# All 128 chunks of U computed ahead of V in the PEER layer

## The chip, the cores and the metric

The kernel runs on one core of a Trainium2 chip. Time is device microseconds; the time given for a kernel is the median over its runs. A profile is one more execution, taken with the hardware profiler. The engines are PE (TensorE, the matmuls; PEld is its weight loading), DVE (VectorE), ACT (ScalarE), POOL (GpSimd) and SP (SyncE, which here only issues DMAs).

## The reference, cut to what matters

The whole computes two blocks of a network on 512 tokens of width 1024: a mixer (neighbourhood attention and a gated linear recurrence) and a PEER layer, and then a second block of convolution, attention and two feed-forward layers. The change is in the PEER layer, with one piece in the mixer. In the PEER layer each token chooses, in each of 8 heads, 16 of 16384 experts by product keys, and sums their outputs:

```python
q = (t @ wq).reshape(PEER_BLOCK, PEER_HEADS, 2, PEER_DQ // 2)
s = jnp.einsum('tpcd,pckd->tpck', q, sub_keys).astype(jnp.float32)
s1, i1 = lax.top_k(s[:, :, 0], PEER_TOPK)
s2, i2 = lax.top_k(s[:, :, 1], PEER_TOPK)
...
top, pos = lax.top_k(cand, PEER_TOPK)
idx = jnp.take_along_axis(cidx, pos, axis=-1)
g = jax.nn.softmax(top, axis=-1)
a = jax.nn.gelu(jnp.einsum('tpkd,td->tpk', u[idx], t).astype(jnp.float32), approximate=False)
return jnp.einsum('tpk,tpkd->td', (g * a).astype(t.dtype), v[idx])
```

## The kernel before, in words

The first 128 tokens (`T0`) are done as the reference says, by gathering: for every token the rows of U, and then of V, of its 128 experts are fetched. POOL issues an indirect DMA for 128 rows of 4 KB (one expert of each token, 512 KB), and DVE multiplies it with the token's input and sums (U, line 1155), or adds it, weighted, to the output `accg` (V, line 1160). There are 256 such tiles, five buffers for them (`GBUFS`), and each is asked for three ahead of its use.

The other 384 tokens (`TD`) are done densely. The experts lie in 128 chunks of 128. For chunk e, `hidden` (line 1335) loads U's part of 512 KB on SP's queue into one of four `w` buffers, splits it into a high and a low half (ACT makes `wh`, DVE `wl`), and makes 24 matmuls of 384 columns: three products (high by high, high by low, low by high) for each of eight pieces of the contraction. ACT takes the GELU of the result, the tile `act`, 128 x 384. For the second half of the layer, `operands` (line 1360) multiplies `act` by the routing weights of the chunk (`Wr`, on DVE), splits the result (`sh`, `sl`), loads V's part of 512 KB into a `w` buffer and splits it (`vh`, `vl`). `products` then makes 18 matmuls of 512 columns into six banks of PSUM that gather the sum over all chunks.

The order is this. While the routing is computed (`route`: `topk`, mostly DVE, and `spread`, which builds for each of the 384 tokens a matrix of routing weights with small matmuls and stores them to DRAM as `Wd`), PE computes U's chunks ahead of need: `ahead` computes `AHEAD` = 116 chunks and stores each `act` to DRAM (`Ad`, line 1357, on ACT's queue). `weave` (line 64) decides the order by costs: it always takes the next step of that generator whose summed costs are smallest. A step of `ahead` costs `PACE` = 2.95, a step of `spread` 1.45, two gathered tiles `GATHER` = 11; `topk` of one block of 128 tokens comes to 47.6, `spread` of one to 46.4. `merge` joins the `topk` of block t and the `spread` of block t-1, and their costs add up. `REST` = 4 of the 116 chunks come after the weave. PE's order is the one written there; on the other engines and on SP's queue a planner orders the instructions by their place in the program and by when it expects them to be ready.

Then comes the V stage (the loop in `peer`, line 1064 on): for e from 0 to 127 the operands, a share of the gathering that is left (spread over the first 120 chunks), and the products of chunk e - `OPS_LAG` (2). For e below 116 the `act` is loaded back from `Ad` (line 1368), into one of three buffers; the last 12 chunks call `hidden` there. `Wr` holds the weights of `GROUP` = 8 chunks. It is loaded whole at the first chunk of a group, 1536 KB in pieces of 512 bytes (line 1365), into one of two buffers. The split halves have `TAIL + OPS_LAG` = 4 buffers each. The last two chunks' products are held back and made bank by bank.

Three more things are touched. `late_mods` computes the columns of four modulation vectors on DVE (`mod_chunk`, line 324, from 32 parts of `wmt` loaded on SP's queue through the `w` buffers), while the mixer's first projection runs on PE. `rows_of` (line 363) makes of such a column vector a row that lies in all 128 partitions, by multiplying the identity with it on DVE (`dg`) and with a matrix of ones on PE. And the layer's input, `h2` (32 KB of each partition), lies lowest on the right side of SBUF until the V stage is done, because `hidden` is still called there; what the gathering needs (`pg`) lies above it, and the V stage's pool `pm` above that.

## Time and profile before

| | |
|---|---|
| median of 3 runs | 3147.87 us (3142.14 to 3153.35) |
| the profiled execution | 3142.09 us, of which its span is 3140.3 us |
| mean granted clock of TensorE | 0.974 |
| PE, PEld | busy 94% and 81% of the span |
| DVE, ACT, POOL | busy 60%, 40%, 13% |
| DMA | 537.8 MB, mean 171 GB/s |

The page cuts the span into 40 equal slices, 78.5 us each. PE counts as busy also where a matmul waits in its pipeline, so the steps between the starts of matmuls say more. A DMA share of 1.00 means that the core's 16 DMA engines were busy all the time; packets that overlap can bring it above. In the view by stretches, a number in brackets is the count of instructions. A line as `1601.98 0.96 PE ... x2 [3.57 <-ACT vh L132]` means two instructions from 1601.98 us on, ahead of which the engine was idle for 3.57 us, until ACT's `vh` released it.

### The profile page before, as it was taken

The page shows a single profiled execution, that of the slowest core. Times are in us where ns is not written, and L with a number is a line of the kernel's source. Part 1 is how long each engine was busy: PE and PEld are TensorE (multiplying, and loading weights), DVE is VectorE, ACT ScalarE, POOL GpSimd, SP SyncE. Part 2 cuts the span into 40 slices and gives each one's busy share as a digit, 9 for nine tenths or more (in the row PEclk, how much of TensorE's full clock was granted, in tenths as well). Part 3 has the DMA queues.
Part 4 walks back from the last instruction along what each step waited for, and adds up shares of the span by engine and source line. Part 5 has one row for each costly group of instructions (what it writes and reads, how often), then busy time and mean ns, then how long its engine had stood idle before and what let it go on. Part 6 is the DMA issues. An engine that isn't in the chain of part 4 may idle for free.

```text
span 3140.3 us, 42392 instructions
## 1 busy us (share of the span) xinstructions
PE 2951.1 (94%) x16073; PEld 2529.5 (81%) x16073; DVE 1898.6 (60%) x3680; ACT 1268.6 (40%) x2275; POOL 401.1 (13%) x398
## 2 busy tenths in 40 slices
PE   7998999999999999898888888899999999999998
PEld 5887887799899999776676767778888887788887
DVE  5744497549999856678788875544433245543323
ACT  4233463343466778522232323432423234433222
POOL 2100000001111110133344431000000000000000
PEclk9999999999999999999999998999999999999999
DMA  6622202236676776899999995222333322123332
GB/s 250 228 64 72 62 1 81 98 126 202 204 239 218 255 248 225 286 353 358 355 363 360 361 353 201 64 72 94 100 95 94 99 86 65 54 88 94 99 103 81
DMA packets 257166, 537.79 MB, mean 171 GB/s; under 512 B 20161, under 2 KB 135105, under 8 KB 252609
## 3 DMA queue, kind: packets, MB, share of 16 engines
q1 hardware_dynamic: 196512, 345.82, 33.8%
q0 software_dynamic: 36864, 134.23, 12.0%
q10 hardware_dynamic: 23584, 55.03, 4.6%
q8 instruction: 126, 2.06, 0.3%
q14 instruction: 80, 0.65, 0.1%
HBM read 484.93 MB, written 50.08 MB: 170 GB/s over the span
## 4 chain that ended last, share of the span: by engine, by line
PE 56%; DVE 19%; DMA 9%; issue 4%; ACT 1%; POOL 1%; SPq 0%; DVEq 0%; ACTq 0%; POOLq 0%
PE bank L121 54%; DMA act<-Ad 7%; DVE wl L1343 2%; DVE gr L1155 2%; DVE accg L1160 2%; DVE vl L134 2%; DVE sl L134 1%; PE bank L608 1%; DVE act L1372 1%; PE bank L1471 1%; DVE idx L1275 1%; DVE tmp L1233 1%; DVE eq L1272 1%; DVE eq L1274 1%; DVE KX L802 1%
## 5 line engine op out<-in xcount | busy, mean ns | idle before, releaser
L121 PE MATMUL bank<-hh,wl 128*128 128x512 f32 (+2 forms) x2304 | 837.0, 364 | 41.8 <-DVE wl L1343 32.3
L121 PE MATMUL bank<-hh,wh 128*128 128x512 f32 (+2 forms) x2304 | 843.0, 367 | 16.2 <-ACT wh L1342 6.8
L121 PE MATMUL bank<-hl,wh 128*128 128x512 f32 (+2 forms) x2304 | 834.5, 362 | 1.5 <-DVE hl L271 0.8
L148 DVE TENSOR_TENSOR wl<-w,wh 128x1024 fp32r<-128x1024 f32 (+2 forms) x280 | 295.0, 1054 | 644.2 <-ACT wh L147 637.5
L147 ACT ACTIVATE wh<-w 128x1024 fp32r<-128x1024 f32 (+2 forms) x280 | 257.5, 920 | 746.1 <-PE bank L121 604.1
L121 PEld LDWEIGHTS bank<-hh,wl 128*128 128x128 f32 x2304 | 437.9, 190 | 101.0 <-DVE wl L1343 42.6
L121 PEld LDWEIGHTS bank<-hh,wh 128*128 128x128 f32 x2304 | 438.1, 190 | 69.9 <-ACT wh L1342 7.6
L121 PEld LDWEIGHTS bank<-hl,wh 128*128 128x128 f32 x2304 | 438.4, 190 | 48.9 <-DVE hl L532 1.6
L121 PE MATMUL bank<-vh,sh 128*128 128x512 f32 x768 | 248.7, 406 | 45.9 <-ACT sh L132 30.8
L121 PE MATMUL bank<-vl,sh 128*128 128x512 f32 x768 | 249.6, 407 | 19.4 <-DVE vl L134 19.2
L1136 POOL DMA_INDIRECT gr<-in_Un_dram,iu x128 | 170.6, 1333 | 735.7 <-DVE accg L1160 493.2
L121 PE MATMUL bank<-vh,sl 128*128 128x512 f32 x768 | 244.3, 400 | 0.0
L132 ACT ACTIVATE sh<-act 128x384 fp32r<-128x384 f32 x128 | 67.1, 525 | 383.4 <-DVE act L1372 347.3
L121 PEld LDWEIGHTS bank<-vh,sh 128*128 128x128 f32 x768 | 149.2, 196 | 80.6 <-ACT sh L132 33.8
L1343 DVE TENSOR_TENSOR wl<-w,wh 128x1024 fp32r<-128x1024 f32 x128 | 156.1, 1221 | 77.3 <-ACT wh L1342 77.3
L1342 ACT ACTIVATE wh<-w 128x1024 fp32r<-128x1024 f32 x128 | 135.1, 1056 | 163.8 <-PE bank L121 144.0
L121 PEld LDWEIGHTS bank<-vl,sh 128*128 128x128 f32 x768 | 149.1, 196 | 59.5 <-DVE vl L134 28.8
L121 PEld LDWEIGHTS bank<-vh,sl 128*128 128x128 f32 x768 | 150.4, 196 | 32.9 <-DVE sl L134 0.2
L1136 POOL DMA_INDIRECT gr<-in_V_dram,iv x128 | 151.4, 1183 | 172.4 <-DVE gr L1155 105.5
L134 DVE TENSOR_TENSOR vl<-w,vh 128x1024 fp32r<-128x1024 f32 x128 | 156.6, 1223 | 13.4 <-ACT vh L132 13.1
L1160 DVE SCALAR_TENSOR_TENSOR accg<-gr,wt,accg 128x1024 f32<-128x1024 f32 x127 | 162.8, 1282 | 0.2 <-DMA gr<-in_V_dram,iv 0.2
L1155 DVE SCALAR_TENSOR_TENSOR gr<-gr,h 128x1024 f32<-128x1024 f32 x128 | 156.0, 1221 | 2.8 <-DMA gr<-in_Un_dram,iu 2.8
(373 smaller groups left out, 4690.9 us busy)
## 6 DMA issues: line engine op xcount, KB each, us to landing
w<-in_U_dram SPq DMA_DIRECT2D x128, 512.0 KB, 4.6
w<-in_V_dram SPq DMA_DIRECT2D x128, 512.0 KB, 6.9
w<-in_wgu_dram SPq DMA_DIRECT2D x84, 512.0 KB, 3.5
Wd<-W ACTq DMA_DIRECT2D x24, 1024.0 KB, 6.8
Wr<-Wd SPq DMA_DIRECT2D x16, 1536.0 KB, 17.6
w<-in_wdown_dram SPq DMA_DIRECT2D x44, 512.0 KB, 3.6
Ad<-act ACTq DMA_DIRECT2D x116, 192.0 KB, 3.7
act<-Ad SPq DMA_DIRECT2D x116, 192.0 KB, 6.5
```

Of the source, the lines that this page charges most:

```text
L121: return self.nc.tensor.matmul(out, a, b, start=start, stop=stop)
L132: self.nc.scalar.activation(hi, src, AF.Copy)
L134: (low or self.nc.vector).tensor_tensor(out=lo, in0=src, in1=hi, op=OP.subtract)
L147: self.nc.scalar.activation(hi[:, :, :n], w[:, :, :n], AF.Copy)
L148: (self.low or self.nc.vector).tensor_tensor(out=lo[:, :, :n], in0=w[:, :, :n], in1=hi[:, :, :n], op=OP.subtract)
L608: nc.tensor.matmul(o, x[k], y[:, kk, :256], start=k == 0 and i == 0 and t % 2 == 0, stop=k == KC - 1 and i == 2, skip_group_check=True)
L802: nc.vector.tensor_tensor(out=half(KX[:, :, l], d), in0=half(e, d), in1=half(kt, d), op=OP.mult)
L1136: nc.gpsimd.indirect_dma_start(out=t, out_offset=None, in_=table, in_offset=bass.IndirectOffsetOnAxis(ap=idx, axis=0))
L1155: nc.vector.scalar_tensor_tensor(t, t, 1.0, self.h0, op0=OP.mult, op1=OP.mult, accum_out=dots[:, h, k:k + 1])
L1160: nc.vector.scalar_tensor_tensor(acc, t, wt[:, h, k:k + 1], acc, op0=OP.mult, op1=OP.add)
L1342: nc.scalar.activation(uh, w, AF.Copy)
L1343: nc.vector.tensor_tensor(out=ul, in0=w, in1=uh, op=OP.subtract)
```

## The change

All 128 chunks of U go into `ahead`, at a pace of 2.66 in the weave, so that 124 of them are spread over the same routing and four follow. No chunk of U is computed in the V stage, and `h2` is closed before it; `pg` moves to the left side, and the V stage's pool begins where `h2` was. In that pool `act` gets six buffers (three before) and the split parts of `act` and of V six (four before); `OPS_LAG` becomes 4. `Wr` is loaded in six pieces of 256 KB, one behind the V load of each of the third to eighth chunk of the group before. `rows_of` no longer computes: `late_mods` stores the four vectors to DRAM (`keep_rows`, on SP's queue, one element of 4 bytes apart), and `rows_of` loads a vector into all partitions.

```diff
--- before.py
+++ after.py
@@ -21,17 +21,19 @@
 FF = 2816
 T0 = 128
 TD = S - T0
-AHEAD = 116
 REST = 4
-PACE = 2.95
+PACE = 2.66
 GROUP = 8
+WLATE = 2
+ABUFS = 6
+VBUFS = 6
 WBUFS = 4
 LAG = 1
 WT = 16
 GBUFS = 5
 GAHEAD = 3
 GATHER = 11.0
-OPS_LAG = 2
+OPS_LAG = 4
 TAIL = 2
 STATE = 3.0
 ATT_LAG = 2
@@ -360,18 +362,14 @@
         self.nc.vector.scalar_tensor_tensor(o, scale[:, :, j], 1.0, self.gains[:, vec], op0=OP.add, op1=OP.mult)
         return o
 
-    def rows_of(self, vec, name, pool):
-
-        nc = self.nc
+    def keep_rows(self, n, vec):
+
+        self.nc.sync.dma_start(self.Rd[n].rearrange("(k p) -> p k", p=128), vec)
+
+    def rows_of(self, n, name, pool):
+
         o = pool.tile([128, D], F32, name=name)
-        for h in range(2):
-            b = self.bank()
-            for q in range(4):
-                k = h * 4 + q
-                dg = pool.tile([128, 128], F32, name="dg", bufs=2)
-                nc.vector.tensor_scalar(dg, self.ident, vec[:, k, 0:1], None, op0=OP.mult)
-                self.mm(b[:, q * 128:(q + 1) * 128], self.ones, dg, True, True)
-            nc.vector.tensor_copy(o[:, h * 512:(h + 1) * 512], b)
+        self.nc.sync.dma_start(o, self.Rd[n].partition_broadcast(128))
         return o
 
 
@@ -465,12 +463,18 @@
                 nc.vector.tensor_tensor(out=f, in0=f, in1=self.lb[:, d:d + 1].to_broadcast([128, 3, 512]), op=OP.add)
 
     def late_mods(self):
+        self.Rd = self.tc.dram_tile([4, D], F32, name="Rd")
         for j, name in ((2, "gt1"), (3, "sh2"), (4, "sc2"), (5, "gt2")):
             t = self.g.tile([128, KC, 1], F32, name=name)
             setattr(self, name, t)
             for k in range(KC):
                 self.mod_chunk(j, t[:, k], k)
                 yield 3.0
+            if j in (2, 3, 5):
+                self.keep_rows((2, 3, 5).index(j) + (j > 2), t[:, :, 0])
+            if j == 4:
+                self.a2 = self.gain_of(1, t, 0, "a2")
+                self.keep_rows(1, self.a2)
 
     def mix_norm(self, hh, hl):
 
@@ -727,7 +731,7 @@
                 self.shut("hcb")
                 self.open_stream()
                 wo = self.pool("wo")
-                self.gate = self.rows_of(self.gt1, "gt1r", ha)
+                self.gate = self.rows_of(0, "gt1r", ha)
                 self.mix_head(wo)
             if i >= 1:
                 self.hg_merge(*units[i - 1], A, X.pop(i - 1)[2])
@@ -1022,8 +1026,7 @@
         nc, p = self.nc, self.p
         hh, hl = self.h2
         mv = ([hh[:, k] for k in range(KC)], [hl[:, k] for k in range(KC)])
-        a2 = self.gain_of(1, self.sc2, 0, "a2")
-        first = self.proj_first(self.ws, mv, lambda i: self.normed_half(i, [(hh, hl, a2)], 1e-6, self.sh2[:, :, 0]))
+        first = self.proj_first(self.ws, mv, lambda i: self.normed_half(i, [(hh, hl, self.a2)], 1e-6, self.sh2[:, :, 0]))
         self.finish = None
         for name in ("wo", "st", "hca", "y", "pn"):
             self.shut(name)
@@ -1032,26 +1035,28 @@
         self.mv = mk.tile([128, 2, 2, C], F32, name="mv")
         self.open_stream()
         self.Wd = self.tc.dram_tile([TD // WT, 128, 128, WT], F32, name="Wd")
-        self.Ad = self.tc.dram_tile([AHEAD, 128, TD], F32, name="Ad")
-        pg = self.pool("pg", "right")
-        self.rows_natural(pg, a2)
+        self.Ad = self.tc.dram_tile([128, 128, TD], F32, name="Ad")
+        pg = self.pool("pg")
+        self.rows_natural(pg)
         sc = self.queries(mv, first)
         pq = self.pool("pq", "right")
-        ac = self.pool("ac")
         pa = self.pool("pa")
         dense = tuple([x[:, T0:] for x in part] for part in mv)
         ahead = self.ahead(pa, dense)
         self.chosen = None
-        gather = self.gathered(pg, ac)
+        gather = self.gathered(pg)
         with self.tc.manual_schedule(engines={mybir.EngineType.PE}):
-            weave(self.route(pq, pg, sc), steps(ahead, AHEAD - REST), self.until_routed(gather))
+            weave(self.route(pq, pg, sc), steps(ahead, 128 - REST), self.until_routed(gather))
         self.shut("pq")
         self.shut("psc")
         run(ahead)
         self.shut("pa")
+        self.shut("h2")
         pm = self.pool("pm", "right")
         ar = self.pool("ar")
-        rows = self.rows_of(self.gt2, "gt2r", ar)
+        for i in range(GROUP - WLATE):
+            self.spread_rows(pm, 0, i)
+        rows = self.rows_of(3, "gt2r", ar)
         banks = [[self.bank() for _ in range(2)] for _ in range(3)]
         ops = {}
         held = []
@@ -1059,7 +1064,7 @@
         done = 0
         for e in range(128 + OPS_LAG):
             if e < 128:
-                ops[e] = self.operands(pm, e, dense)
+                ops[e] = self.operands(pm, e)
             want = left * min(e + 1, 120) // 120
             for _ in range(done, want):
                 next(gather, None)
@@ -1073,8 +1078,7 @@
         run(gather)
         for t in range(3):
             self.products(banks, [t], held)
-        for name in ("pm", "pg", "h2"):
-            self.shut(name)
+        self.shut("pm")
         pt = self.xp = self.pool("pt", "right")
         nf = pt.tile([128, D], F32, name="nf")
         nc.scalar.dma_start(nf, self.rowb(p['normf'], D))
@@ -1097,14 +1101,14 @@
                 self.square_sum(self.X[:, t, hs], ss[:, t, h:h + 1], pt.tile([128, 512], F32, name="sqx", bufs=2))
             self.unit(t, 1e-5, 4)
         self.shut("ar")
-        self.shut("ac")
-
-    def rows_natural(self, pg, a2):
+        self.shut("pg")
+
+    def rows_natural(self, pg):
 
         nc = self.nc
         self.h0 = h = pg.tile([128, D], F32, name="h0")
         tmp = self.pool("rn")
-        gain, shift = self.rows_of(a2.unsqueeze(2), "a2r", tmp), self.rows_of(self.sh2, "sh2r", tmp)
+        gain, shift = self.rows_of(1, "a2r", tmp), self.rows_of(2, "sh2r", tmp)
         r = self.rstd(self.ss[:, 0], 1e-6)
         nc.vector.scalar_tensor_tensor(h, self.X[:, 0], r, gain, op0=OP.mult, op1=OP.mult)
         nc.gpsimd.tensor_tensor(out=h, in0=h, in1=shift, op=OP.add)
@@ -1121,14 +1125,14 @@
             n += 1
         self.gather_left = (256 + GAHEAD) // 2 - n
 
-    def gathered(self, pg, ac):
+    def gathered(self, pg):
 
 
         nc, p = self.nc, self.p
         iu, iv, g = self.chosen
-        dots = ac.tile([128, 8, 16], F32, name="dots")
-        wt = ac.tile([128, 8, 16], F32, name="wt")
-        self.accg = acc = ac.tile([128, D], F32, name="accg")
+        dots = pg.tile([128, 8, 16], F32, name="dots")
+        wt = pg.tile([128, 8, 16], F32, name="wt")
+        self.accg = acc = pg.tile([128, D], F32, name="accg")
         ring = {}
 
         def load(key, table, idx):
@@ -1352,29 +1356,36 @@
         return a
 
     def ahead(self, pool, mv):
-        for e in range(AHEAD):
+        for e in range(128):
             a = self.hidden(pool, e, mv)
             self.nc.scalar.dma_start(self.Ad[e], a)
             yield PACE
 
-    def operands(self, pm, e, mv):
+    def operands(self, pm, e):
 
         nc, p = self.nc, self.p
-        if e % GROUP == 0:
-            self.Wr = pm.tile([128, TD // WT, GROUP, WT], F32, name="Wr", bufs=2)
-            nc.sync.dma_start(self.Wr, self.Wd[:, :, e:e + GROUP, :].rearrange("b p e t -> p b e t"))
-        if e < AHEAD:
-            a = pm.tile([128, TD], F32, name="act", bufs=3)
-            nc.sync.dma_start(a, self.Ad[e])
-        else:
-            a = self.hidden(pm, e, mv)
+        n, j = divmod(e, GROUP)
+        if j == 0:
+            self.Wr = self.Wn
+        a = pm.tile([128, TD], F32, name="act", bufs=ABUFS)
+        nc.sync.dma_start(a, self.Ad[e])
         a3 = a.rearrange("p (b t) -> p b t", t=WT)
         self.anchor = nc.vector.tensor_tensor(out=a3, in0=a3, in1=self.Wr[:, :, e % GROUP], op=OP.mult)
-        sh, sl = self.split(pm, a, [128, TD], "s", bufs=TAIL + OPS_LAG)
+        sh, sl = self.split(pm, a, [128, TD], "s", bufs=VBUFS)
         v = self.st.tile([128, 2, 512], F32, name="w", bufs=WBUFS)
         nc.sync.dma_start(v.rearrange("p a b -> p (a b)"), p['V'][e])
-        vh, vl = self.split(pm, v, [128, 2, 512], "v", bufs=TAIL + OPS_LAG)
+        if j >= WLATE and e < 128 - GROUP:
+            self.spread_rows(pm, n + 1, j - WLATE)
+        vh, vl = self.split(pm, v, [128, 2, 512], "v", bufs=VBUFS)
         return sh, sl, vh, vl
+
+    def spread_rows(self, pm, n, i):
+
+        if i == 0:
+            self.Wn = pm.tile([128, TD // WT, GROUP, WT], F32, name="Wr", bufs=2)
+        m = TD // WT // (GROUP - WLATE)
+        bs = slice(i * m, i * m + m)
+        self.nc.sync.dma_start(self.Wn[:, bs], self.Wd[bs, :, n * GROUP:(n + 1) * GROUP, :].rearrange("b p e t -> p b e t"))
 
     def products(self, banks, tiles, ops):
```

## Rows read from the trace of the kernel before

**Rows 1.** Page, megabytes moved per second, in 40 slices of 78.5 us.

```profile
GB/s 250 228 64 72 62 1 81 98 126 202 204 239 218 255 248 225 286 353 358 355 363 360 361 353 201 64 72 94 100 95 94 99 86 65 54 88 94 99 103 81
```

**Rows 2.** By stretch: length, PE, PEld, DVE, ACT, POOL, clock, DMA share, GB/s.

```profile
1351.40:1384.00 32.60, 32.60 (x145) 27.00 (x144) 28.32 (x38) 10.46 (x14) 12.75 (x11) 1.00 1.01 362
...
1426.50:1467.40 40.90, 35.47 (x146) 28.39 (x145) 33.13 (x45) 11.91 (x17) 15.64 (x15) 0.92 1.00 357
...
1831.50:1874.80 43.30, 34.33 (x146) 27.99 (x145) 34.53 (x47) 12.55 (x18) 16.63 (x15) 0.92 0.99 348
1874.80:1953.50 78.70, 65.25 (x314) 58.58 (x313) 45.45 (x49) 25.02 (x32) 15.26 (x9) 0.89 0.67 227
1953.50:2007.20 53.70, 53.70 (x265) 47.65 (x263) 26.90 (x37) 18.94 (x31) 0.98 (x3) 1.00 0.33 104
sum 690.30, PE 611.51 PEld 501.70 DVE 528.30 ACT 208.88 POOL 244.68; mean PE 38.22 PEld 31.36 DVE 33.02 ACT 13.05 POOL 15.29
```

**Rows 3.** Waits, 1340 to 1870 us: total, times, longest.

```profile
DVE act L1372 <- DMA act<-Ad: 99.9, 16, 8.8
```

**Rows 4.** PE's timeline at a stall; in brackets the idle time before.

```profile
1601.98 0.96 PE L121 MATMUL bank<-vh,sh 128*128 128x512 f32 x2 [3.57 <-ACT vh L132]
...
1605.30 1.06 PE L121 MATMUL bank<-vh,sl 128*128 128x512 f32 x2
1606.16 1.06 PE L121 MATMUL bank<-vh,sh 128*128 128x512 f32 x2
```

**Rows 5.** By stretch, two moments of the V stage, columns as rows 2.

```profile
1599.00:1602.00 3.00, 0.02 (x1) 0.03 (x1) 2.27 (x4) 1.47 (x2) 0.25 (x1) 1.00 1.03 401
...
1629.00:1632.00 3.00, 3.00 (x15) 2.49 (x14) 3.00 (x5) 1.48 (x2) 2.35 (x2) 1.00 1.19 292
```

**Rows 6.** SP's timeline, issues of Wr and of the act behind it.

```profile
1294.18 0.38 SPq L1365 DMA_DIRECT2D Wr<-Wd  x1
...
1622.49 0.37 SPq L1365 DMA_DIRECT2D Wr<-Wd  x1
1624.57 6.55 SPq L1368 DMA_DIRECT2D act<-Ad  x2
```

**Rows 7.** By stretch, U stage and what follows, columns as rows 2.

```profile
689.00:835.00 146.00, 136.98 (x770) 132.21 (x769) 145.73 (x555) 52.43 (x70) 14.91 (x12) 1.00 0.58 186
835.00:1010.40 175.40, 166.20 (x1022) 164.25 (x1021) 174.83 (x580) 118.19 (x229) 24.18 (x17) 0.98 0.69 231
1010.40:1177.40 167.00, 164.29 (x1039) 163.23 (x1039) 118.50 (x153) 117.83 (x227) 25.12 (x18) 1.00 0.73 246
1177.40:1285.10 107.70, 102.59 (x644) 97.28 (x642) 69.28 (x96) 87.58 (x194) 10.45 (x8) 1.00 0.63 220
...
1301.60:1316.90 15.30, 3.17 (x13) 2.34 (x12) 10.82 (x20) 4.42 (x7) 3.89 (x4) 0.62 1.03 386
```

**Rows 8.** PE's timeline late in the U stage.

```profile
1283.04 0.34 PE L121 MATMUL bank<-hl,wh 128*128 128x384 f32 x1
1283.21 0.34 PE L121 MATMUL bank<-hh,wl 128*128 128x384 f32 x1
1283.39 1.95 PE L121 MATMUL bank<-go,oh 128*128 128x128 f32 x16
```

**Rows 9.** Groups by line, DVE, 1296 to 2004 us: busy, mean ns, idle before.

```profile
L1160 DVE SCALAR_TENSOR_TENSOR accg<-gr,wt,accg 128x1024 f32<-128x1024 f32 x112 | 143.6, 1282 | 0.2 <-DMA gr<-in_V_dram,iv 0.2
L1155 DVE SCALAR_TENSOR_TENSOR gr<-gr,h 128x1024 f32<-128x1024 f32 x95 | 116.0, 1221 | 0.0
```

**Rows 10.** PE's waits, 1296 to 2004 us: total, times, longest.

```profile
PE bank L121 <- DVE dg L372: 12.1, 2, 11.4
```

**Rows 11.** Instructions on the tile dg: ns least, median, most.

```profile
L121 PE MATMUL bank<-dg,ones x64: 270/275/581, 492.5 to 1320.6; 128*128 128x128 f32 x64
```

**Rows 12.** Issues of line 329, the loads of wmt.

```profile
DMA to landing us min/median/max: 3.5/4.7/12.0
```

**Rows 13.** By stretch, in late_mods, columns as rows 2.

```profile
100.00:140.00 40.00, 38.03 (x210) 31.16 (x209) 34.73 (x72) 8.47 (x14) 0.00 (x0) 1.00 0.85 290
```

## The prediction

> **What bounds the kernel now.** I read the page's slices first. One band stands out, slices 18 to 24 of 78.5 us each (1335 to 1884 us): 353 to 363 GB/s, above all that lies beside it [rows 1]. That is the V stage, so I cut it at every eighth V chunk. From the third group on, twelve groups in a row take 39 to 43 us each, 40.8 in the middle, at DMA share 1.0 and about 357 GB/s (the second and the last of the twelve are shown); the one before them took 32.6 us. PE has 144 matmuls in each, 0.226 us apart in the quick one, and its clock is 0.92 in the slow ones against 1.00 [rows 2]. The last two groups are of another kind: 78.7 and 53.7 us at DMA shares of 0.67 and 0.33. There the 12 chunks of U that were not computed ahead are computed between the V chunks, on PE, while the transfers idle. The waits say where a slow group loses its time: DVE waits 99.9 us in 16 waits for `act<-Ad` [rows 3], and PE behind DVE. One such stall, in PE's timeline: a gap of 3.57 us, a shorter one, and then matmuls 0.43 us apart, half the clock (1.2 for 2.4 GHz) [rows 4]. SP's queue has the reason: the next group's whole `Wr`, 1536 KB, is issued ahead of the `act` load that DVE needs next [rows 6].
>
> The U stage is bounded differently: DVE is busy without a gap up to 1010 us, PE after that [rows 7].
>
> **Term 1, the U stage gets 12 chunks more.** A U chunk is 24 matmuls that start 0.173 us apart [rows 8], 4.16 us of PE. The stretches of rows 7 begin at chunks 0, 32, 64, 96 and 112 of the weave, which follow from its costs: 95.2, 94, 94 and 46.4 units of routing at 2.95 a chunk. At 2.66 they hold 35.8, 35.3, 35.3 and 17.4 chunks; four more follow the weave in both kernels. One step of `spread` is 8 matmul records of 0.11 to 0.12 us [rows 8], 0.9 us, 32 steps in each of the last three stretches.
> - 689 to 835 us: PE needs 32 x 4.16 = 133 of 146 us, DVE 145.7. The 3.8 chunks more cost DVE 1.22 us each (the `wl` split, of the size of the other 128x1024 operations on DVE [rows 9]), 4.6 us, and PE 15.8 us of which 13 were idle. Between 4.6 and 15.8, I take 6, since DVE is the fuller.
> - 835 to 1010: PE needs 133 + 29 = 162 of 175.4, DVE 174.8. Between 4 and 14; I take 9.
> - 1010 to 1177: PE 162 of 167, DVE 118.5. Between 9 and 14; 13.
> - 1177 to 1285: 95 of 107.7; 1.7 chunks, 7 us of PE, into 12 us of idle: between 2 and 7; 6.
>
> Sum +34 us; ends +20 and +50 (12 x 4.16 us).
>
> **Term 2, the V stage.** A group moves 8 V parts of 512 KB (4.19 MB), 8 `act` of 192 KB (1.57 MB), one `Wr` (1.57 MB), and gathered rows: 112 + 95 = 207 tiles of 512 KB in the stage [rows 9], spread over 120 chunks, so 13.8 a group, 7.23 MB. That makes 14.57 MB, and over 40.8 us 357 GB/s, as the rows say. So the stall is no mere wrong order: the transfers are busy all the time, and spreading `Wr` removes none of their bytes. What it can win is rate. While PE stands still and every queue has work, the rate is 401 GB/s; in the stretch 7 us behind the issue of a `Wr`, 292 [rows 5, 6]. At these two, a group needs 13.0/401 + 1.57/292, 37.8 us. PE needs 32.7 and DVE about 33 [rows 2], so neither comes first. Floor 37.8, ceiling 40.8 (nothing gained). With twice the `act` buffers, `Wr` in six pieces and six parts of s and V in place of four, more loads stand in the queue at any time, but the rows gathered keep their five buffers, and DVE takes them in order: I take 39.
>
> Afterwards there are 15 such groups and one (chunks 120 to 127, no gather) at PE's own 32.7. The first groups before ran at PE's pace on a lead: transfers began at 1294 [rows 6], 23 us ahead of the first V matmul at 1316.9. That lead shrinks. The pool of the V stage now lies where the layer's input was (the right side's lowest place), so whichever of its tiles come there, `Wr` first as I read the order, can't be loaded before the last U matmul has read it. I leave 6 us of lead (between 0 and 15). From the first V matmul to the last: 15 x 39 - 6 + 32.7 = 612 us, against 690.3 before (the sum of all sixteen stretches in [rows 2]). That is -79; ends -99 (37.8) and -46 (40.8 and no lead). Most of it, -61, needs no theory of transfers: the last two groups took 132.4 us and would take 39 + 32.7.
>
> **Term 3, between the stages.** From the last U matmul to the first V matmul it was 15.3 us [rows 7], 12.1 of them PE's waits for `dg`, the diagonal tiles of `rows_of` [rows 10]. These are gone. What is late next: `Wr`, six issues and 1.57 MB, 5.4 us at 292 GB/s, then an `act`, and DVE's and ACT's work on it of about half a microsecond each. I estimate 10 us, -5; ends -8 and +8. It matters little that `gt2r` is now a load in SP's queue behind them: it is read at the end only.
>
> **Term 4, the rows.** The other three `rows_of` cost PE some 5 us in matmuls (48 of 64 records [rows 11], 0.11 us each as in `spread`); waits for `dg` may come to a few more, and some of it lies in PE's idle time, so between 0 and -8. I take -7. Against it stand the four stores of `keep_rows` in SP's queue at 60 to 135 us. Each waits for DVE's last column, and behind it wait the loads of the next `wmt` and `win` parts. A part lands 4.7 us after issue [rows 12], so a queue that ran empty costs up to that, four times; the cover is PE's work on weights already there, 38 of 40 us busy [rows 13]. Between 0 and +15; +5. Together -2.
>
> **Sum.** 34 - 79 - 5 - 2 = -52 us. The profiled execution took 3142.1 us (span 3140.3); it would take 3090. The median of the runs shown is 5.8 us higher, so the forecast for the median is 3147.9 - 52 = 3096.
>
> **Rivals.**
> - *The rate is capped.* A group stays at 40.8 us, since 357 GB/s is all that a long stretch gets: 15 x 1.8 = +27, 3123 us. For it: twelve groups in a row come to about this rate [rows 2]. Against it: 401 GB/s when the queues are full [rows 5]. The Trainium skill, "DMA: Bandwidth & Descriptors", section Specifications, gives a limit of about 358 GB/s of HBM for each core, which is this stage's mean; the trace goes above it for microseconds, and no row shows it for longer.
> - *The buffers aren't filled.* SP issues in order, `act` of e+1 stands behind V of e, and that waits for one of four `w` slots, whose number is unchanged. If `act` still comes late once a group, the stall and its 40.8 us remain: 3123 us again. Against it: a lead of four chunks, 16 us, against three before, and pieces of 256 KB in place of 1536 KB.
> - *Slower: PE's clock.* Once transfers pace every chunk, PE waits a little in each rather than once in eight, and its clock may stay at half, as after the stall: 18 x 0.43 = 7.7 us [rows 4] a chunk for 4.08. With n such chunks a group takes 32.7 + 3.6 n. It decides from n = 3: 43.5 us, +68 on the forecast, 3164 us. For it: one in eight is slow already. Against it: a slow chunk lets the buffers fill, and the following run at full clock; in the U stage PE lacks up to 9 us in 175 in short pieces, at a clock of 0.98 to 1.00 [rows 7]. The Trainium skill, "TensorE: Matmul & The Clock Gate", section HAM oscillation, describes a kernel that pays for the clock at each wait for a DMA; here the trace agrees for the waits once a group.
>
> **Chances.** The forecast (group 37.8 to 40) 0.60, with 3070 to 3115 as its own range; the cap 0.20; the unfilled buffers 0.12; the clock 0.05; anything else 0.03. The range takes the two cases at 3123 in, and the ends of terms 1 and 4: 3068 to 3131. No change means within 0.3%, 9.4 us, what a measurement here can't tell apart. The forecast and both cases at 3123 lie 25 us and more below the old median; a U stage at its full 50 us or the stores of `keep_rows` on top of them would bring the time into the band. So faster 0.88, same 0.06, slower 0.06.
>
> **What would show it.** The last U matmul at about 1335 us of the span rather than 1301.6; no stretch of V with DMA at 0.33 except the last 33 us; groups of 39 us with rates near 375 GB/s and DVE waits for `act<-Ad` far below 100 us; the first V matmul about 10 us after the last U. It is wrong if groups keep 40.8 us or pass 42, if the granted clock in V falls below 0.92, if the U stage grows by over 50 us, or if PE gets a gap between 100 and 150 us.

## The result, and the profile after

The changed kernel takes 3191.6 us (median; 3188.01 to 3196.34), the kernel before 3148.79 (3142.14 to 3153.35): 1.0139 times as long, interval 1.0115 to 1.0162. The forecast was 3096. The profiled execution took 3189.84 us with a span of 3188.1, 47.8 us more than before. Cut at the same events, the two spans differ so:

| | before | after | difference | forecast |
|---|---|---|---|---|
| first instruction to the first U matmul | 688.9 | 726.5 | +37.6 | -2 |
| first to last U matmul | 612.8 | 657.0 | +44.2 | +34 |
| to the first V matmul | 15.2 | 10.9 | -4.3 | -5 |
| V stage | 690.3 | 653.8 | -36.5 | -79 |
| behind the V stage | 1133.1 | 1139.9 | +6.8 | 0 |

The page after, its engines' busy time and the GB/s of its 40 slices (79.7 us each):

```profile
PE 2964.2 (93%) x16009; PEld 2523.4 (79%) x16009; DVE 1890.3 (59%) x3640; ACT 1268.4 (40%) x2275; POOL 452.4 (14%) x398
...
GB/s 254 183 71 69 82 15 60 113 113 136 222 224 218 248 250 242 208 308 364 335 344 372 346 331 350 162 62 104 86 99 93 100 93 67 47 86 99 93 106 80
```

Against [rows 1] the band of the V stage is no longer even at 353 to 363 GB/s: it goes from 331 to 372, and its mean is lower. By stretch (length, PE, PEld, DVE, ACT, POOL with counts, clock, DMA share, GB/s): five stretches of the U stage and the gap behind it.

```profile
726.50:888.00 161.50, 155.13 (x863) 149.58 (x862) 159.69 (x603) 58.05 (x78) 19.82 (x15) 0.99 0.60 195
888.00:1073.70 185.70, 177.76 (x1100) 174.85 (x1100) 185.29 (x558) 123.85 (x237) 21.96 (x14) 1.00 0.66 223
1073.70:1250.00 176.30, 176.30 (x1110) 176.30 (x1109) 107.69 (x138) 120.59 (x232) 25.19 (x18) 1.00 0.74 245
1250.00:1366.70 116.70, 109.79 (x688) 105.49 (x687) 70.51 (x98) 90.70 (x197) 11.63 (x8) 0.99 0.63 216
1366.70:1383.40 16.70, 16.70 (x99) 16.63 (x98) 3.60 (x4) 5.30 (x8) 0.00 (x0) 1.00 0.86 275
1383.40:1394.40 11.00, 0.26 (x2) 0.00 (x0) 5.79 (x7) 4.84 (x7) 0.00 (x0) 0.70 0.83 242
```

They answer to [rows 7]. There the first two stretches are cut a fraction of a chunk earlier than here; cut at the same chunks (after 32.3, 64.1 and 96.0 of 116, as here after 35.8, 71.1 and 106.5 of 128) the first three of the kernel before are:

```profile
688.90:837.80 148.90, 138.58 (x778) 133.49 (x777) 148.53 (x563) 53.86 (x72) 16.73 (x13) 1.00 0.58 187
837.80:1010.80 173.00, 165.10 (x1017) 163.47 (x1016) 172.41 (x572) 117.14 (x228) 22.37 (x16) 0.98 0.69 231
1010.80:1177.40 166.60, 163.90 (x1037) 162.83 (x1036) 118.11 (x152) 117.45 (x227) 25.12 (x18) 1.00 0.73 247
```

Groups of eight V chunks, two slow ones, the quickest of the third to the fourteenth and the last, answer to [rows 2]:

```profile
1509.10:1550.70 41.60, 35.26 (x146) 27.86 (x144) 32.85 (x45) 12.01 (x16) 20.32 (x15) 0.92 0.97 343
1550.70:1594.20 43.50, 36.32 (x145) 27.09 (x145) 33.73 (x47) 12.12 (x17) 20.46 (x15) 0.96 0.96 334
1720.10:1758.60 38.50, 34.08 (x146) 26.45 (x144) 33.30 (x46) 12.00 (x16) 20.91 (x14) 1.00 1.04 382
2014.90:2048.20 33.30, 32.89 (x145) 26.76 (x143) 20.70 (x28) 10.55 (x14) 0.00 (x0) 1.00 0.50 154
```

The third to the fourteenth group take 42.2 us in the mean, not 39. Their waits (1410 to 1970 us: total, times, longest) show what took the place of [rows 3]:

```profile
ACT vh L134 <- DMA w<-in_V_dram: 344.3, 100, 9.2
...
DVE sl L136 <- ACT sh L134: 111.8, 45, 6.2
...
PE bank L123 <- ACT sh L134: 80.0, 39, 6.3
```

DVE waits for ACT's `sh`, and so does PE; ACT itself waits for V's loads with `vh`. ACT's timeline, in brackets the idle time ahead of the instruction and who ended it, says how one makes the other:

```profile
1593.61 0.51 ACT L134 ACTIVATE sh<-act 128x384 fp32r<-128x384 f32 x1
1600.36 1.06 ACT L134 ACTIVATE vh<-w 128x1024 fp32r<-128x1024 f32 x1 [6.24 <-DMA w<-in_V_dram]
1601.32 0.51 ACT L134 ACTIVATE sh<-act 128x384 fp32r<-128x384 f32 x1
1608.73 1.06 ACT L134 ACTIVATE vh<-w 128x1024 fp32r<-128x1024 f32 x1 [6.91 <-DMA w<-in_V_dram]
1609.70 0.51 ACT L134 ACTIVATE sh<-act 128x384 fp32r<-128x384 f32 x1
```

ACT stands at `vh` for 6.24 and 6.91 us, and each `sh` behind it in ACT's order runs the moment that `vh` is through. The two do not belong to one chunk: the first `vh` here is chunk 43's (counted from 0) and the `sh` behind it chunk 41's. Over chunks 64 to 111 `vh` starts 12.4 us ahead of the first matmul that reads it, and `sh` 0.7 us ahead of its own (medians; before it was 5.0 and 3.6). So a V part that nobody needs for 12 us holds up the `sh` that PE needs now.

The first 37.6 us lie in `late_mods`. The stores of `keep_rows`, and the DMA of the stretch behind the first of them (packets; queue with its share of the 16 engines; loads with their median us to landing):

```profile
L367 SPq DMA_DIRECT2D Rd<-gt x2: 381/401/421, 87.4 to 170.8; - x2
L367 SPq DMA_DIRECT2D Rd<-sh x1: 378/378/378, 118.8 to 118.8; - x1
L367 SPq DMA_DIRECT2D Rd<-a x1: 378/378/378, 143.5 to 143.5; - x1
```

```profile
DMA packets 1288, 0.88 MB, mean 68 GB/s; under 512 B 1065, under 2 KB 1065, under 8 KB 1288
...
q1 hardware_dynamic: 1288, 0.88, 52.8%
...
w<-in_wmt_dram SPq DMA_DIRECT2D x3, 512.0 KB, 14.7
```

A store of 4 KB is 1024 packets of 4 bytes. From 88 to 101 us the core moves 68 GB/s, and the loads of `wmt` issued then land after 14.7 us, against 4.7 in [rows 12]. DVE now loses 33.5 us to these loads (55 to 230 us; before, the first line, 9.1), and PE is 65% busy in 100 to 120, at a clock of 0.74, where [rows 13] showed 38.03 of 40 us:

```profile
DVE mscr L331 <- DMA w<-in_wmt_dram: 9.1, 9, 2.0
```

```profile
DVE mscr L333 <- DMA w<-in_wmt_dram: 33.5, 9, 10.7
```

```profile
100.00:120.00 20.00, 12.98 (x47) 10.02 (x48) 14.11 (x28) 6.50 (x11) 0.00 (x0) 0.74 0.74 251
140.00:160.00 20.00, 8.94 (x75) 7.69 (x75) 9.60 (x21) 2.35 (x4) 0.00 (x0) 0.81 0.82 200
```

### The profile page after: what moved, and what is told of

It is laid out like the page before. It is cut to its first block, busy times and chain, and to the rows that moved or that the text cites. A ratio compares the mean times of both kernels' runs of the same rounds, so it can differ in the third digit from the quotient of the medians.

```text
span 3188.1 us, 42344 instructions
## 1 busy us (share of the span) xinstructions
PE 2964.2 (93%) x16009; PEld 2523.4 (79%) x16009; DVE 1890.3 (59%) x3640; ACT 1268.4 (40%) x2275; POOL 452.4 (14%) x398
## 3 DMA queue, kind: packets, MB, share of 16 engines
q1 hardware_dynamic: 204256, 350.30, 34.4%
## 5 line engine op out<-in xcount | busy, mean ns | idle before, releaser
L123 PE MATMUL bank<-hh,wh 128*128 128x512 f32 (+2 forms) x2304 | 843.6, 367 | 19.5 <-ACT wh L149 10.7
L1140 POOL DMA_INDIRECT gr<-in_Un_dram,iu x128 | 206.6, 1614 | 833.0 <-DVE accg L1164 578.5
L134 ACT ACTIVATE vh<-w 128x1024 fp32r<-128x1024 f32 x128 | 135.4, 1060 | 377.9 <-DMA w<-in_V_dram 376.9
L1140 POOL DMA_INDIRECT gr<-in_V_dram,iv x128 | 166.9, 1304 | 72.7 <-DVE accg L1164 34.0
L217 POOL TENSOR_TENSOR r<-r,mhalf 128x1 f32<-128x1 f32 x37 | 22.0, 597 | 983.1 <-DVE r L216 976.1
```

Of the source, the lines that this page charges most:

```text
L123: return self.nc.tensor.matmul(out, a, b, start=start, stop=stop)
L134: self.nc.scalar.activation(hi, src, AF.Copy)
L217: nc.gpsimd.tensor_tensor(out=r, in0=r, in1=self.mhalf[:, :1], op=OP.pow)
L1140: nc.gpsimd.indirect_dma_start(out=t, out_offset=None, in_=table, in_offset=bass.IndirectOffsetOnAxis(ap=idx, axis=0))
```

## The experiments

Two theories were to be tested: that the stores of `keep_rows` cost the 37.6 us, and that ACT's order (`vh` ahead of an older `sh`) keeps the V stage from what the transfers allow. The rivals: that the stores only stand in the wrong queue, that the U stage grew for another reason than its 12 chunks, and that 42 us a group is all that the memory gives.

**Rows by matmuls.** The changed kernel, with `rows_of` as before and no stores.

```diff
-            if j in (2, 3, 5):
-                self.keep_rows((2, 3, 5).index(j) + (j > 2), t[:, :, 0])
             if j == 4:
                 self.a2 = self.gain_of(1, t, 0, "a2")
-                self.keep_rows(1, self.a2)
...
-        self.nc.sync.dma_start(o, self.Rd[n].partition_broadcast(128))
...
+                dg = pool.tile([128, 128], F32, name="dg", bufs=2)
+                nc.vector.tensor_scalar(dg, self.ident, vec[:, k, 0:1], None, op0=OP.mult)
+                self.mm(b[:, q * 128:(q + 1) * 128], self.ones, dg, True, True)
...
```

> The changed kernel, but the four vectors stay in SBUF and rows_of makes its rows with matmuls as before; keep_rows and its DRAM tile are gone. Theory (stores): the 37.6 us that the changed kernel lost before its first U chunk are owed to the four stores of 1024 single elements in SP's queue; the first U matmul comes back to 689 us of the span, give or take 3, and the time falls by 35 to 40 us, to about 3153 us. Rival (order): the planner's new order on SP and DVE did it, by the other edits of late_mods (gain_of moved there) or by the pools that moved; then the first U matmul stays past 715 us and the time within 10 us of 3192.

Measured: 3150.13 us, ratio to before 1.0012 (0.9999 to 1.0024). The first U matmul is back at 690.1 us. The U stage (657.0) and the V stage (651.8 to the start of its last matmul, 653.6 in the changed kernel; the V times below are cut alike) stay as they were. In the stretch 88 to 101 us:

```profile
DMA packets 1176, 3.39 MB, mean 261 GB/s; under 512 B 96, under 2 KB 96, under 8 KB 1175
...
w<-in_wmt_dram SPq DMA_DIRECT2D x5, 512.0 KB, 4.6
```

The stores cost what was lost ahead of U. Without them the rest of the change nets nothing.

This run also shows what the `dg` waits between the stages were worth. The matmuls of `rows_of` are back there, and PE waits for `dg`; in the changed kernel it waits for `sh` (1344 to 1360 us here, 1380 to 1396 there):

```profile
PE bank L123 <- DVE dg L374: 6.5, 3, 5.2
```

```profile
PE bank L123 <- ACT sh L134: 10.7, 1, 10.7
```

Yet from the last U matmul to the first V matmul it takes 11.3 us here and 11.1 there (start to start). The first `sh` is done at 1357.3 us here, 0.9 us ahead of that V matmul, so the `dg` waits lie within the wait for the first loads, and dropping them is not what shortened the 15.3 us of before. There the first `dg` began 11.3 us behind the last U matmul, here 5.1.

**The stores on ACT's queue.**

```diff
-        self.nc.sync.dma_start(self.Rd[n].rearrange("(k p) -> p k", p=128), vec)
+        self.nc.scalar.dma_start(self.Rd[n].rearrange("(k p) -> p k", p=128), vec)
```

> The changed kernel with the four stores issued on ACT's queue, not on SP's. If the loads were late because they stood behind the stores in one queue, they pass now: first U matmul at 685 to 700 us, time near 3155 us. If the 16 DMA engines themselves are held up by 1024 writes of 4 bytes, whatever queue they come from, the loads stay late: first U matmul at 715 to 730 us, time near 3190 us.

Measured: 3179.8 us, ratio 1.0115 (1.0089 to 1.0141), first U matmul at 716.7. Of the 37.6 us, 10 come back. The DMA from 84 to 98 us, around the first store, which is now in another queue (q10) than the loads (q1):

```profile
q1 hardware_dynamic: 565, 1.32, 36.5%
q10 hardware_dynamic: 923, 0.00, 3.5%
...
w<-in_wmt_dram SPq DMA_DIRECT2D x4, 512.0 KB, 12.4
...
Rd<-gt ACTq DMA_DIRECT2D x1, 4.0 KB, 13.0
```

The store is issued at 90.1 us and lands at 103.1. One of the four loads is issued ahead of it and lands after 3.6 us; the three behind it, in the other queue, land after 12.1, 12.7 and 13.4 us. By stretch, ahead of the store, while it runs and behind it (the last two columns are the DMA share and GB/s):

```profile
87.00:90.00 3.00, 3.00 (x18) 2.42 (x17) 2.90 (x6) 1.12 (x3) 2.88 (x3) 1.00 0.00 0
93.00:100.00 7.00, 7.00 (x41) 6.10 (x40) 1.54 (x4) 0.56 (x1) 0.00 (x0) 1.00 0.35 34
103.00:106.00 3.00, 0.13 (x1) 0.14 (x1) 1.39 (x3) 1.22 (x2) 0.00 (x0) 0.85 1.01 394
```

So the order in SP's queue is the smaller part, about 10 of the 37.6 us; a store of 4-byte pieces slows the transfers beside it. By what it does so isn't settled: some 900 of its 1024 packets lie between 91 and 93 us, their own time is 3.5% of the engines, and the loads stay slow for 7 us more.

**Stores in pieces of 32 bytes.** Each partition writes its eight values side by side, 128 pieces for 1024. The rows then hold the columns in another order, so the output is another one; the work is the same.

```diff
-        self.nc.sync.dma_start(self.Rd[n].rearrange("(k p) -> p k", p=128), vec)
+        self.nc.sync.dma_start(self.Rd[n].rearrange("(p k) -> p k", p=128), vec)
```

> The changed kernel, with each vector stored as it lies, 32 bytes of each partition in one piece: 128 pieces, not 1024. The rows read back have their elements in another order, so this run's output is another one. If the count of pieces is the price, a store lands in about 3 us rather than 10 to 12, and the first U matmul is at 685 to 700 us. If the price is SP's wait for DVE ahead of the store, it stays past 715 us.

Measured: 3149.84 us, ratio 1.0017 (1.0003 to 1.0031), first U matmul at 687.0; the stores land after 2.9 to 3.7 us, for 10.0 to 12.4. The same bytes in the same queue behind the same waits, an eighth of the pieces: the loss is gone. The price hangs on the pieces; with the bytes fixed, their number and their size go together and the run doesn't part them. It also gives a bound on the matmuls that the loads replace: 687.0 against 690.1, one profile each. The eight kernels profiled here that make their rows by matmuls begin U at 688.9 to 693.1, so that is some 2 to 6 us, and the two medians (3149.84 and 3150.13) show nothing of it.

**All chunks ahead, nothing else.** The kernel before with two constants changed.

```diff
-AHEAD = 116
+AHEAD = 128
-PACE = 2.95
+PACE = 2.66
```

> The kernel before with two constants changed: 128 chunks ahead, at a pace of 2.66; Wr, the buffers, h2 and rows_of as before. Theory: the U stage grows by 44 us, as in the changed kernel (each chunk costs nearly its whole 4.16 us of PE), the V stage loses its last 59 us (two groups at 40.8 and 32.7 us in place of 132.4), so the net is -15 us, 3134 us. Rival: the V groups before needed the quiet end to work off what was late; then their mean rises above 42 us and the time is 3149 us or more.

Measured: 3146.46 us, ratio 1.0003 (0.9988 to 1.0018). U 655.4 us (+42.6), V 639.0 (-51.0), the gap between them 19. The U stage grows by the same 42 to 44 us without the new pools, so it is the 12 chunks. I had expected 3134: V's last two groups do give back 57 us, but its third to fourteenth come to 41.4 us in the mean for 40.9 (6 us in all), and the gap grows by 4. So moving U alone gains nothing. `Wr` still comes whole, `act` has three buffers, and the old stall stands: DVE waits 115.1 us for `act<-Ad` (1400 to 1960 us).

The next kernels all start from the one with rows by matmuls (3150.13 us), so that the stores don't blur V. They ran on another chip than it; the kernel before took 3146.35 us on its chip and 3144.77 and 3146.94 on theirs, so a difference of some 2 us to 3150.13 means nothing.

**`sh` ahead of `vh`.** ACT may not start `vh` of a chunk until `sh` of that chunk is done. Nothing else is touched in the program; the planner orders the rest around this rule.

```diff
-        sh, sl = self.split(pm, a, [128, TD], "s", bufs=VBUFS)
+        sh = pm.tile([128, TD], FR, name="sh", bufs=VBUFS)
+        first = nc.scalar.activation(sh, a, AF.Copy)
...
-        vh, vl = self.split(pm, v, [128, 2, 512], "v", bufs=VBUFS)
+        vh = pm.tile([128, 2, 512], FR, name="vh", bufs=VBUFS)
+        with self.after(first):
+            nc.scalar.activation(vh, v, AF.Copy)
...
```

> The kernel x1 (the changed kernel with rows by matmuls), and on ACT the split of V of chunk e may not be put ahead of the split of act of the same chunk. In x1 ACT's queue has vh of later chunks ahead of sh, vh waits for V's load (315 us in 91 waits), and DVE (109.5 us) and PE (75.7) wait for the sh behind it. Theory (ACT's order): with sh first DVE's wait for sh goes, the V groups fall from 42.2 to 39 to 40 us and the time by 25 to 40 us, to about 3115. Rival (transfers): V's loads come late because the queues carry all they can; the wait moves to vl or act, the groups stay at 41 to 42.5 us and the time within 8 us of 3150.

Measured: 3104.88 us, ratio 0.9879 (0.9863 to 0.9896). V takes 599.8 us for 651.8, its first fifteen groups 37.8 in the mean. ACT's waits for V in the kernel that it starts from (1400 to 1930 us) and here (1432 to 1929), and three of its groups by stretch:

```profile
ACT vh L134 <- DMA w<-in_V_dram: 315.3, 91, 10.1
```

```profile
ACT vh L1384 <- DMA w<-in_V_dram: 59.6, 21, 5.9
```

```profile
1509.40:1545.90 36.50, 34.98 (x145) 26.41 (x144) 32.92 (x47) 12.04 (x17) 14.34 (x14) 1.00 1.05 391
1545.90:1583.80 37.90, 35.11 (x145) 26.41 (x145) 33.60 (x46) 11.93 (x16) 14.15 (x15) 1.00 1.05 388
1583.80:1621.20 37.40, 34.92 (x146) 26.50 (x145) 33.58 (x48) 12.70 (x19) 13.72 (x15) 1.00 1.05 389
```

ACT's wait for V falls from 315.3 us to 59.6, and PE no longer waits for `sh` (75.7 us before the edit). The transfers of the changed kernel from 1400 to 1970 us, and here from 1400 to 1930:

```profile
DMA packets 101301, 198.94 MB, mean 349 GB/s; under 512 B 7808, under 2 KB 63272, under 8 KB 101270
```

```profile
DMA packets 102280, 202.02 MB, mean 381 GB/s; under 512 B 7938, under 2 KB 63610, under 8 KB 102245
```

The rival that memory gives no more is out.

**Four buffers for V's parts.** `vh` and `vl` with four for six, so that ACT can't go as far ahead.

```diff
-        vh, vl = self.split(pm, v, [128, 2, 512], "v", bufs=VBUFS)
+        vh, vl = self.split(pm, v, [128, 2, 512], "v", bufs=4)
```

> The kernel x1 with four buffers for vh and vl, as before the change (six for sh and sl). Theory (ACT's order): vh can't run ahead of PE by more than four chunks, so it waits for PE rather than for V's load, sh stands behind it for less, and the groups come to 40 to 41 us: time 3125 to 3140. Rival (transfers): no change, 41 to 42.5 us a group, 3150.

Measured: 3125.37 us, ratio 0.9945 (0.9928 to 0.9962). Fewer buffers, 25 us quicker. ACT's wait for V's loads is 212.3 us in 63 times (1405 to 1940 us). Of the 45 us that the right order gives, 25 come from merely limiting the wrong one: the extra room for V's parts let `vh` run ahead.

**`Wr` whole.** One load of 1536 KB behind the last V load of the group before, in place of six of 256 KB.

```diff
-        if j >= WLATE and e < 128 - GROUP:
-            self.spread_rows(pm, n + 1, j - WLATE)
+        if j == GROUP - 1 and e < 128 - GROUP:
+            self.spread_rows(pm, n + 1, 0)
...
```

> The kernel x1, with Wr of the next group loaded whole (1536 KB in one issue) behind the last V part of a group, not in six pieces. If the six pieces help against the burst, this is slower: the stall once a group is back with act or V late, groups of 43 to 45 us, 3165 to 3190. If the transfers bound the stage whatever their order, it is the same within 8 us as 3150.

Measured: 3184.01 us, ratio 1.0126 (1.0109 to 1.0143); one chunk of 11 to 16 us in all but one of the third to the fifteenth group, and 326 GB/s (1437 to 2016 us). Loading `Wr` in pieces, the first of them five chunks earlier than this whole load, is worth some 34 us here, under the wrong order of ACT; pieces and earlier start aren't parted. It is the one part of the change that worked against the old stall as meant.

**More gathered in the U stage.** `GATHER` 6 for 11, so that 42 tiles more (96 for 54) are fetched ahead of V.

```diff
-GATHER = 11.0
+GATHER = 6.0
```

> The kernel x1 with GATHER = 6 in place of 11: the weave puts about 94 of the 256 gathered tiles into the U stage, not 52, and 165 are left for the V stage, 11 a group and 13.1 MB in place of 14.6. Theory (transfers bound V): groups fall in proportion, 42.2 to about 38 us, the V stage by some 55 us; the U stage pays 15 to 30 us where DVE is full (up to about 1000 us of the span), for 42 tiles of 1.25 us; net -25 to -40, 3110 to 3125. Rival (ACT's order bounds V): groups stay above 41 us, and the U stage's price makes it slower, 3165.

Measured: 3161.0 us, ratio 1.0058 (1.0036 to 1.008). U takes 16 us more; V's first six groups take 33 to 38 us, the next eight, from about 1590 us on, 41 to 50. The theory (3110 to 3125) missed and the rival came: alone it does not help.

**The order in the changed kernel as it is,** stores included.

> The changed kernel as it is, stores of keep_rows included, with one edit: ACT's vh of a chunk is kept behind sh of the same chunk. Theory (two causes that add up: the stores hold the DMA engines in late_mods, ACT's order starves V): the first U matmul stays near 726 us, the V stage falls from 653.8 to about 600, and the whole comes to about 3190 - 45 = 3145 us. Rival (the gain of the order belongs to the kernel with the matmul rows only): the V stage stays above 640 and the time above 3180.

Measured: 3139.22 us, ratio 0.9978 (0.9965 to 0.9991); first U matmul at 726.3, V 599.2 us against 653.6. The two causes add up as expected: 52 us quicker than the changed kernel with one order fixed, and 34 us slower than the same without the stores.

**The order with more gathered in the U stage,** `GATHER` 6 and 8.

> Rows by matmul and sh ahead of vh (3104.9 us), and the gather's cost in the weave 6 for 11: by the trace of the same edit alone, 39 tiles of 512 KB more are gathered in the U stage, which grows by 18 us. Theory (with ACT's order mended, the transfers bound V: 381 GB/s over twelve groups of 37.7 us): 1.33 MB less a group, 34.7 us in place of 37.7, V about 45 us shorter, 3078 us in all; if DVE or PE come first at 34 to 36 us a group, 3085 to 3095. Rival (the order of the gathers on DVE and POOL bounds the groups, as with the edit alone, whose groups after 1590 us took 45 us at 291 GB/s): V no shorter than 585 us and 3110 or more.

> The same with the gather's cost 8 for 11, about half of the move. Transfers as the bound: U +9, groups near 36 us, 3090 us. The rival: 3105 or more.

Measured: 3155.49 us (ratio 1.003, 1.002 to 1.004) and 3110.83 (0.988, 0.9862 to 0.9898). Both miss my theory. (The expectation's 39 tiles are 42, as above; with 8 it is 20.) With 6, V's groups take 32.6 to 35.1 us up to 1575 us, better than I expected, and then 38 to 52 at a rate far below what the memory gives. By stretch, before and behind that point:

```profile
1440.00:1590.00 150.00, 144.88 (x631) 117.59 (x629) 128.31 (x178) 50.55 (x70) 53.04 (x49) 1.00 1.05 385
1590.00:1960.00 370.00, 304.22 (x1190) 235.54 (x1191) 254.60 (x338) 101.73 (x143) 112.21 (x88) 0.93 0.87 295
```

Behind 1590 us the loads of `act` are issued 5.2 us ahead of their use (median of chunks 64 to 111), against 23.8 with 11; and ACT stands 39.9 us, in four waits, at `wt`, the small activation between the two halves of the gathering, with `vh` and `sh` behind it. The waits (1430 to 1980 us) name what costs most:

```profile
DVE act L1373 <- DMA act<-Ad: 119.5, 58, 8.9
...
PE bank L123 <- DVE vl L1386: 66.8, 41, 7.1
```

This is the same stall on another engine. `sh` now starts 19.4 us ahead of its first matmul (same chunks; 2.9 with 11), so the `act` for which DVE stands belongs to a chunk that PE reaches much later, while the `vl` that PE needs now stands behind it: at 1775 us DVE waits 4.09 us for chunk 89's `act`, with chunk 84's `vl` behind it and PE at chunk 84. Why the planner's order turns there is open. With 8, V is 19 us shorter, but U 29 us longer where I allowed 9 (PE waits 34.4 us there for `wl`, 17.1 with 11).

**Room for the tail.** After V, the pool of the next part lay in the place of V's pool. Here it lies below it; for the room, `vh` and `vl` have four buffers.

```diff
+        pt = self.pool("pt", "right")
         pm = self.pool("pm", "right")
...
-        pt = self.xp = self.pool("pt", "right")
+        self.xp = pt
...
```

> Rows by matmul and sh ahead of vh (3104.9 us), and the pool for what follows the V stage lies below V's pool rather than in its place (for the room, vh and vl have four buffers for six). Theory (after V, y waited for PE's last reads of V's buffers): from the last V matmul to PE's last 1124 us as before, not 1131, and y of the first 128 tokens starts some 8 us ahead of V's end; with V unchanged 3098 us. If four buffers of V's parts are too few, V grows from 600 by up to 20 and the end from V on still shows 1124. Rival (the 7 us come from elsewhere): 1131 stays.

Measured: 3095.35 us, ratio 0.9838 (0.9818 to 0.9857), the quickest of all. From the last V matmul to PE's last it is 1120.3 us for 1130.8 with the order alone, 1131.0 with four buffers alone, 1130.9 in the changed kernel and 1124.2 before. So it is the pool's place and not the buffers; why it comes out 4 us below the kernel before is open. What DVE waited for at that point of the changed kernel, and the instructions that read the gathered sum, in the changed kernel and here (count, ns, first and last start; the last V matmul is at 2048.0 and at 1963.7):

```profile
2046.62 1.29 DVE L1094 TENSOR_TENSOR y<-accg,gt2r 128x512 f32<-128x512 f32 x2 [11.74 <-PE bank L123]
```

```profile
L1094 DVE TENSOR_TENSOR y<-accg,gt2r x2: 687/690/692, 2046.6 to 2047.2; 128x512 f32<-128x512 f32 x2
```

```profile
L1095 DVE TENSOR_TENSOR y<-accg,gt2r x2: 685/690/695, 1943.7 to 1944.3; 128x512 f32<-128x512 f32 x2
```

They start 20 us ahead of V's end, not with it (7.6 us ahead in the kernel before), and wait for no matmul. With `sh` ahead of `vh`, four buffers cost V some 5 us (605.1 against 599.8).

## Why the prediction was wrong

- **Term 4.** The step that failed is "a part lands 4.7 us after issue, so a queue that ran empty costs up to that, four times": +5, at most +15, for what cost about 39 (726.5 us against 687.0 with 32-byte pieces). Two of the prediction's own signs of being wrong came: PE's gap between 100 and 150 us here, and groups of over 42 us in term 2. I priced the stores as places in SP's queue. The two ACT-queue and 32-byte kernels show that the place is the smaller part (10 us) and the 1024 pieces the larger: loads beside a store land after 12 to 15 us. The pieces stood in the diff ("one element of 4 bytes apart"), and I gave them no price. The Trainium skill, "DMA: Bandwidth & Descriptors", states both halves of what I left out: in section Rules for kernel authors, that a last dimension that isn't contiguous becomes one descriptor per element, and in section Issuing engines are not separate DMA queues, that DMAs of all issuing engines run on the same 16 DMA engines. The runs agree: some 1024 packets of under 512 bytes to a store, and 12 to 13 us for loads beside it in another queue. The other half, -7 for the matmuls that go, measured some -2 to -6.
- **Term 2, the largest miss,** -79 forecast, -36.5 measured. The working was right as to bytes and rate: the floor of 37.8 us a group is what the kernel with `sh` ahead of `vh` nearly reaches (38.0 from the third to the fourteenth, 37.8 over the first fifteen). The lower end of -99 does not follow from its terms (37.8 a group with 6 us of lead gives -97, with 15 us -106); nothing hangs on it. The step that failed is "with twice the `act` buffers ... more loads stand in the queue": I asked only what fills the queues, not what six buffers of `vh` allow ACT to do ahead of need. The stall moved from `act<-Ad` to `sh` behind `vh`. Of my rivals, the cap at 357 GB/s falls by the traces: 382 GB/s over a group of 38.5 us in the changed kernel, 381 over 530 us with the order mended. (That no row showed more than 358 for longer is misread: [rows 7] has 386 over 15.3 us.) The Trainium skill, "DMA: Bandwidth & Descriptors", section Specifications, gives about 358 GB/s as a limit for one core, and its section Bandwidth says that this is what each of two streaming cores gets. With one core at work, the kernel with the order mended goes above it for 530 us. The unfilled buffers had nearly the right price (40.8 us a group; the first fifteen came to 41.4, the third to the fourteenth to 42.2) for the wrong reason: `act` was loaded 26 us ahead of its use. PE's clock did not decide: 0.92 to 1.00 in the groups.
- **Term 1, +34 forecast, +44.2 measured,** inside the ends. The stretches grew by 12.6, 12.7, 9.7 and 9.0 us for 6, 9, 13 and 6. PE's busy time rose by 48.8 us, the 50 of twelve chunks; of 26 us of idle only 5 were filled, where I had counted on 16. The step that failed is PE's idle time: I took what the steps' costs leave over (13 us in the first stretch, 44 in the four) where [rows 7] show 26. In the stretches where DVE is busy to the end, I took DVE's cost as the bound (1.22 us a chunk), and the stretch grew nearly by PE's. Idle time that comes from waits in an order written by hand wasn't free room for more of the same engine's work; which waits keep it open I did not test.
- **Term 3** came as forecast, 10.9 us against 10, but half by luck. The chain that it named as next, `Wr`, `act`, DVE, ACT, is what PE waits for (10.7 us for `sh`). That the `dg` matmuls had to go for it is not so: with them back it is 11.3 us. With the old pools and `Wr` whole it is 19.4, so the gain lies in the other edits; in which one is open.
- **Left out: the tail,** +6.8. I had followed where V's pool goes, at its start, and not which pool takes its place at its end.

So the change was worth -4.3 and -36.5 where it gained, and its U chunks, stores and tail took 88.6. The summed loss has two causes that are shown by single edits (the pieces of the stores; ACT's order), and both mended, with the tail, give 3095.35 us, 51.6 us less than the kernel before on the same chip. What stays open: how 1024 small pieces slow transfers of other queues, why the planner's order turns bad with more gathered ahead, and which edit shortened the gap between the stages.

## What to carry to other kernels

Count a transfer's pieces, not only its bytes and its place in a queue: four 4 KB stores in 4-byte pieces cost some 39 us, beside loads that PE needed, and in 32-byte pieces nothing that could be seen. More buffers let an in-order engine run ahead with the wrong work; ask of each queue which instruction could stand at its head waiting for a load while a later one is needed sooner, and keep the urgent one ahead. And ask of a pool that moves what will lie in its place when it closes.

## What the runs showed of the hardware that I had not expected

One core drew 381 GB/s in the mean for 530 us, in a mix of loads in pieces of 512 bytes and more and gathered rows of 4 KB. A store of 1024 pieces of 4 bytes landed after 10 to 13 us, and while it ran, 512 KB loads issued in another engine's queue took 12.1 to 13.4 us for 4.7; some 900 of its packets lay within 2 us, and for the 7 us behind these the core moved 34 GB/s; once it had landed, 394.
